# Splitting hid once and using more seven-product pairs in an encoder block's channel mixer

## The chip, the cores and the metric

The kernel runs on one core of one Trainium2 chip. The time is the device time of one execution in microseconds (us); several executions are taken and the median is given. A core has TensorE (PE, matrix products; PEld is its weight load), VectorE (DVE), ScalarE (ACT), GpSimd (POOL), a sequencer that here issues almost all DMAs (SP), and 16 DMA engines. Engines work side by side, each through its own instructions in a fixed order, and wait for each other by semaphores. Operands lie in SBUF, 128 partitions wide; PE writes to PSUM, whose banks hold 512 float32 columns.

## The reference

One layer of an encoder on 256 positions of width 2048, all float32. The two parts that the change touches most are the channel mixer and the norm behind it:

```
hn = rmsnorm(h, ffn_norm_pre)
up = hn @ w_ffn_up                        # 2048 -> 2 x 5632
gate, val = split(up)
gate = dwconv_centred(gate, 3 taps, bias) # along positions
ff = (gelu(gate) * val) @ w_ffn_down      # 5632 -> 2048
h = h + rmsnorm(ff, ffn_norm_post)        # rmsnorm: y * rsqrt(mean(y*y) + EPS) * g
```

Ahead of it stand a combined input projection, a bidirectional state-space mixer beside a pooling mixer, and an output projection (w_out), with norms around them. Behind it stands a gate: `h + rmsnorm(sigmoid(rmsnorm(h) @ w_gate) * (p @ w_ple))`.

## The kernel before

**Products in three parts.** To keep float32 accuracy at the speed of a reduced format, each operand is split into a high part (a rounding copy on ACT, `split`, line 149) and a low part (the rest, a subtraction on DVE, line 150). A product is then high x high + high x low + low x high: three matmuls. Weights come from HBM by DMA in pieces of 1 MB into one of three `raw` buffers of 2048 columns, are split 1024 columns at a time into one of five `whi` and five `wlo` buffers, and used once.

**Stages.** In order: dtu, xbc and z (the input projection, with the state-space and pooling work put between its matmuls), wo (the output projection), ple (the small projection of p; its first half here), up, down (called dn), ple's second half, and gt (the gate).

**up.** `feature_pairs` makes 256 of the 5632 gate or value features for all 256 positions. Per k (128 of the 2048 input rows) and per 128 features there is one matmul of 512 columns (the high weight against both parts of the input) and one of 256 (the low weight against the high part). `total` adds the two halves of each bank. A slab is 512 gate and 512 value features; there are 11. After a slab's gate features come `conv` (three taps: one ACT and two DVE instructions for each 128 features), gelu on ACT, and a multiplication by the row scale `rfb` on POOL (line 781), because the pre-norm's row scale is applied behind the projection. The products gate x value go to six pages `hid` in float32.

**down.** `sublayer` runs two halves of 1024 output columns. `token_major` walks through 22 pairs of row blocks (2 x 128 rows of w_down). An ordinary pair has 24 matmuls of 512 columns. For the pairs named in `fast` it calls `seven_products`: a 2 x 2 block product with seven block products in place of eight (21 matmuls), for which DVE makes sums and differences of the weight blocks, and `hid_sums` those of hid. hid is split again in each half, pair by pair (`get_hid`, lines 797 and 798); the sums of four pairs are kept from the first half to the second, the others are made anew. The four accumulators of the ordinary products are in `acc`, those of the shared block products in `alt`; `combine` adds them after the last seven-product pair. At the end of a half, ACT squares each accumulator (for the norm) and DVE multiplies it by the gain; after both halves POOL makes the row scale, DVE adds to the residual `h` (line 740), and PE turns the result for the gate's products (`panel_part`).

**What sets the order.** The program names engines and data; a planner puts the instructions of every engine, and SP's DMAs, into one fixed order by its own estimate of times, with program order as the priority, and hands out buffers as they come free. So the split of a later weight piece can stand ahead of or behind the work of a handover. `load` puts a DMA behind the last weight load, unless it is called with `ahead`.

**Room.** 13 pages of 2048 columns, 3 buffers `mid` of 1024, 6 PSUM banks handed out singly (`main`) and 2 more (`misc`).

## Time and profile before

| what | value |
|---|---|
| median of 3 runs | 1144.95 us (1144.41 to 1144.95) |
| profiled execution's span | 1144.3 us |
| mean granted TensorE clock | 0.994 of full speed |
| busy: PE, PEld, DVE, ACT, POOL | 1127.1, 970.4, 818.4, 614.2, 79.3 us |
| DMA moved | 219.04 MB, mean 191 GB/s |

| stretch, us from the span's start | stage |
|---|---|
| 0 to 53 | dtu |
| 53 to 150 | xbc |
| 150 to 206 | z |
| 206 to 296 | wo |
| 296 to 330 | ple's first half, handover to up |
| 330 to 798.6 | up |
| 798.6 to 1031.5 | down |
| 1031.5 to 1052 | handover to the gate |
| 1052 to 1144.3 | gate and output |

The profile shows one execution. A group's row gives the number of instructions, their busy time and the mean of one in ns, then the time that the engine was idle just before them and what ended it. A row of the timeline gives start and duration. Ends of matmuls are modelled, so a matmul's duration in a row is longer than the pace at which they follow each other; pace is read from starts. A table by stretches gives the busy time of each engine in each, the granted clock, the DMA engines' share and their rate.

### The profile page before, as it was taken

Reading aid. Unit: us, or ns where it says so; the run is one execution under the profiler, and the core shown is the slowest. Engines: PE = TensorE matmul, PEld = TensorE weight load, DVE = VectorE, ACT = ScalarE, POOL = GpSimd, SP = SyncE. Lnnn points to the kernel's source line nnn. Section 1 sums busy time; section 2 is a strip of 40 time slices with the busy share of each in tenths; the row PEclk is TensorE's granted clock in tenths of the full one; section 3 lists DMA queues with packets and bytes.
Section 4 is the critical chain, followed back from the end, with each engine's and each line's share of the span. In section 5 each row is a group of like instructions: output and inputs, shape, how many; then the busy total and the mean of one; then the engine's idle time right before and its main releaser. Section 6 shows DMA issues by size and latency. Waiting matters only on the chain.

```text
span 1144.3 us, 15384 instructions
## 1 busy us (share of the span) xinstructions
PE 1127.1 (98%) x6049; PEld 970.4 (85%) x6049; DVE 818.4 (72%) x1067; ACT 614.2 (54%) x837; POOL 79.3 (7%) x91
## 2 busy tenths in 40 slices
PE   9999999999999999999999999999999999999996
PEld 9998888888888888888888888888888888887885
DVE  6659985754876666665766756668888888898573
ACT  6746543553674554554544545545655655667462
POOL 0201105200110000000000000000000000002001
PEclk9999999999999999999999999999999999999998
DMA  9942366556456555555555555556556746654752
GB/s 357 374 149 74 100 245 221 171 170 198 148 185 214 190 185 184 184 187 194 193 190 193 184 184 184 184 195 220 170 188 220 221 147 221 209 195 147 226 179 74
DMA packets 129592, 219.04 MB, mean 191 GB/s; under 512 B 3696, under 2 KB 96752, under 8 KB 128624
## 3 DMA queue, kind: packets, MB, share of 16 engines
q1 hardware_dynamic: 129232, 217.70, 57.2%
q8 instruction: 47, 0.77, 0.3%
q10 hardware_dynamic: 288, 0.36, 0.1%
q14 instruction: 25, 0.20, 0.0%
HBM read 215.95 MB, written 2.10 MB: 191 GB/s over the span
## 4 chain that ended last, share of the span: by engine, by line
PE 95%; DVE 2%; ACT 1%; POOL 1%; issue 1%; DMA 0%; POOLq 0%; DVEq 0%; ACTq 0%
PE va L86 21%; PE ga L86 21%; PE dna L86 17%; PE woa L86 8%; PE gt L86 7%; PE xbc L86 5%; PE dtu L86 4%; PE z L86 4%; PE dns L86 3%; PE pw L86 1%; PE ple L86 1%; PE yd L86 0%; DVE h L740 0%; PE seg L86 0%; DMA dtur<-w_in 0%
## 5 line engine op out<-in xcount | busy, mean ns | idle before, releaser
L86 PE MATMUL ga<-wox,ug_0h 128*128 128x512 f32 x352 | 125.5, 395 | 0.0
L86 PE MATMUL ga<-wox,ug_1h 128*128 128x512 f32 x352 | 125.1, 394 | 0.0
L86 PE MATMUL va<-wox,uv_0h 128*128 128x512 f32 x352 | 124.8, 393 | 0.0
L86 PE MATMUL va<-wox,uv_1h 128*128 128x512 f32 x352 | 124.8, 393 | 0.0
L86 PE MATMUL ga<-wox,ug_0l 128*128 128x256 f32 x352 | 99.1, 282 | 0.0
L86 PE MATMUL ga<-wox,ug_1l 128*128 128x256 f32 x352 | 99.1, 282 | 0.0
L86 PE MATMUL va<-wox,uv_0l 128*128 128x256 f32 x352 | 99.1, 281 | 0.0
L86 PE MATMUL va<-wox,uv_1l 128*128 128x256 f32 x352 | 99.1, 281 | 0.0
L86 PEld LDWEIGHTS va<-wox,uv_0h 128*128 128x128 f32 x352 | 66.1, 188 | 15.0
L86 PEld LDWEIGHTS va<-wox,uv_1h 128*128 128x128 f32 x352 | 66.1, 188 | 15.0
L86 PEld LDWEIGHTS ga<-wox,ug_1h 128*128 128x128 f32 x352 | 66.1, 188 | 14.9
L86 PEld LDWEIGHTS ga<-wox,ug_0h 128*128 128x128 f32 x352 | 66.1, 188 | 14.8
L86 PE MATMUL dna<-dn_0h,hs 128*128 128x512 f32 x248 | 75.8, 393 | 0.0
L86 PE MATMUL dna<-dn_1h,hs 128*128 128x512 f32 x248 | 75.6, 393 | 0.0
L86 PEld LDWEIGHTS ga<-wox,ug_0l 128*128 128x128 f32 x352 | 66.2, 188 | 0.1
L86 PEld LDWEIGHTS ga<-wox,ug_1l 128*128 128x128 f32 x352 | 66.2, 188 | 0.0
L86 PEld LDWEIGHTS va<-wox,uv_0l 128*128 128x128 f32 x352 | 66.2, 188 | 0.0
L86 PEld LDWEIGHTS va<-wox,uv_1l 128*128 128x128 f32 x352 | 66.2, 188 | 0.0
L781 POOL TENSOR_TENSOR fc<-fc,rfb 128x1024 f32<-128x1024 f32 x11 | 26.5, 2408 | 440.1 <-ACT fc L780 440.1
L86 PEld LDWEIGHTS dna<-dn_1h,hs 128*128 128x128 f32 x248 | 46.5, 188 | 10.8
L86 PEld LDWEIGHTS dna<-dn_0h,hs 128*128 128x128 f32 x248 | 46.5, 188 | 10.7
L86 PE MATMUL dna<-dn_0l,hs 128*128 128x512 f32 x124 | 40.2, 393 | 0.0
(1078 smaller groups left out, 2824.0 us busy)
## 6 DMA issues: line engine op xcount, KB each, us to landing
dn0r<-w_ffn_down SPq DMA_DIRECT2D x22, 1024.0 KB, 5.5
dn1r<-w_ffn_down SPq DMA_DIRECT2D x22, 1024.0 KB, 5.5
zr<-w_in SPq DMA_DIRECT2D x8, 1024.0 KB, 5.1
wo0r<-w_out SPq DMA_DIRECT2D x8, 1024.0 KB, 5.4
wo1r<-w_out SPq DMA_DIRECT2D x8, 1024.0 KB, 5.4
gt0r<-w_ple_gate SPq DMA_DIRECT2D x8, 1024.0 KB, 5.6
gt1r<-w_ple_gate SPq DMA_DIRECT2D x8, 1024.0 KB, 5.5
dtur<-w_in SPq DMA_DIRECT2D x14, 528.0 KB, 8.9
```

The source lines that it names most:

```text
L86: nc.tensor.matmul(o, lhsT, rhs, start=start, stop=stop, skip_group_check=True)
L781: nc.gpsimd.tensor_tensor(cv.rearrange("p (f t) -> p f t", f=4), cv.rearrange("p (f t) -> p f t", f=4), rfb.unsqueeze(1).to_broadcast([P, ...
```

## The change

- **hid.** gate x value goes to a `mid` buffer and is split once, in up, into a high and a low part: five pairs of pages and a smaller pair. `get_hid` is gone. For the pairs that down treats with seven products, DVE makes the sums of hid's blocks in up, too; they are stored to HBM, and each half of down loads and splits them.
- **Pairs.** Every second pair up to the twentieth is a seven-product pair, ten in each half, 20 in all; before it was six and seven. The block sums are taken in another form, into `mid` buffers and not in place.
- **Norm.** The values are no longer multiplied by `rfb`. The row scale of the pre-norm cancels in the norm behind down, except in its EPS, which becomes EPS times the pre-norm's mean square (`fmean`, passed as `base`).
- **Splits.** `whi` and `wlo` are three buffers of 2112 columns, and a 2048-column piece is split in one instruction on each engine; the first piece of a `token_major` stage and of up in steps of 512, 512 and 1024; `feature_major` in two steps as before.
- **Taps.** up's convolution makes its three products on ACT, 12 instructions a slab, and DVE adds them with two instructions of 1024 columns.
- **PSUM.** `main` buffers are pairs of banks, three of them; up's `total` works on 512 columns at once.
- **Room.** 14 pages, 5 `mid` buffers; gains are loaded into pages; h and one half of the gated projection's input are stored to HBM at up's start and loaded again, h at the thirteenth pair of down's second half and the other after down; the scratch space for DMA descriptors is smaller.

```
-            tc.tile_pool(name="pmain", bufs=6, space=bass.MemoryType.PSUM) as pm, \
+            tc.tile_pool(name="dram", bufs=1, space=bass.MemoryType.DRAM) as dp, \
+            tc.tile_pool(name="pmain", bufs=3, space=bass.MemoryType.PSUM) as pm, \
...
-            return gp.tile([P, 2048], dtype, tag="pg", bufs=13, name=name)
+            return gp.tile([P, 2048], dtype, tag="pg", bufs=14, name=name)
...
-            return gp.tile([P, 1024], dtype, tag="mid", bufs=3, name=name)
+            return gp.tile([P, 1024], dtype, tag="mid", bufs=5, name=name)
...
         def main(name):
-            return [pm.tile([P, 512], F32, tag="main", name=f"{name}_{i}") for i in range(2)]
+            t = pm.tile([P, 1024], F32, tag="main", name=name)
+            return [t[:, :512], t[:, 512:]]
...
-        def split(name, src, nel, cuts=()):
+        def parts(name):
             if name in spare:
-                hi, lo = spare.pop(name)
-            else:
-                hi = wp.tile([P, 1056], F32R, tag="whi", bufs=5, name=f"{name}h")
-                lo = wp.tile([P, 1056], F32R, tag="wlo", bufs=5, name=f"{name}l")
-            for c0, c1 in zip((0, *cuts), (*cuts, nel)):
+                return spare.pop(name)
+            return [wp.tile([P, 2112], F32R, tag=tag, bufs=3, name=f"{name}{tag}") for tag in ("whi", "wlo")]
+
+        def split(dst, src, c0, *cuts):
+            hi, lo = dst
+            for c1 in cuts:
                 s = slice(c0, c1)
                 last["act"] = ins(nc.scalar.copy(hi[:, s], src[:, s]))
                 last["dve"] = ins(nc.vector.tensor_sub(lo[:, s], src[:, s], hi[:, s].bitcast(F32)))
+                c0 = c1
...
         def seven_products(name, r, a_, acc, alt, start, stop):
             v = r.rearrange("p (b c) -> p b c", b=4)
-            b11 = split(f"{name}a", r[:, :512], 512)
-            b2 = split(f"{name}b", r[:, 1024:], 1024)
-            nc.vector.tensor_sub(v[:, 0:2], v[:, 1::2], v[:, 0:2])
-            nc.vector.tensor_sub(v[:, 3], v[:, 3], v[:, 0])
-            nc.vector.tensor_sub(v[:, 2], v[:, 2], v[:, 3])
-            t13 = split(f"{name}c", r[:, :1024], 1024)
-            t42 = split(f"{name}d", r[:, 1024:], 1024)
+            f, g = mid(f"{name}f"), mid(f"{name}g")
+            nc.vector.tensor_sub(f.rearrange("p (b c) -> p b c", b=2), v[:, 1:3],
+                                 v[:, 0].unsqueeze(1).to_broadcast([P, 2, 512]))
+            nc.vector.tensor_add(g[:, :512], v[:, 2], f[:, :512])
+            nc.vector.tensor_sub(g[:, 512:], v[:, 3], g[:, :512])
+            b = split(parts(f"{name}b"), r, 512, 2048)
+            t = parts(f"{name}t")
+            for x, c in ((f, slice(0, 1024)), (g, slice(1024, 2048))):
+                split([y[:, c] for y in t], x, 0, 1024)
...
-                for j in range(2):
-                    group.append((k0 + j, *split(f"{name}{k0}_{j}", r[:, j * 1024:(j + 1) * 1024], 1024)))
+                wh, wl = split(parts(f"{name}{k0}"), r, 0, *((512, 1024, 2048) if u == 0 else (2048,)))
+                group.extend((k0 + j, wh[:, j * 1024:(j + 1) * 1024], wl[:, j * 1024:(j + 1) * 1024]) for j in range(2))
...
         def total(o, acc):
-            for f in range(2):
-                nc.scalar.copy(o[:, f * L:(f + 1) * L], acc[f][:, L:])
-                nc.vector.tensor_add(o[:, f * L:(f + 1) * L], o[:, f * L:(f + 1) * L], acc[f][:, :L])
+            v, w = o.rearrange("p (f t) -> p f t", f=2), acc.rearrange("p (f q t) -> p q f t", f=2, q=2)
+            nc.scalar.copy(v, w[:, 1])
+            nc.vector.tensor_add(v, v, w[:, 0])
...
+        def taps(name, x, wcol, bcol):
+            o, t0, t2 = (mid(f"{name}{i}") for i in range(3))
+            for f in range(4):
+                c = slice(f * L, (f + 1) * L)
+                nc.scalar.activation(t0[:, c], x[:, c], AF.Copy, scale=vec(wcol + f))
+                nc.scalar.activation(t2[:, c], x[:, c], AF.Copy, scale=vec(wcol + 2 * NF + f))
+                nc.scalar.activation(o[:, c], x[:, c], AF.Identity, bias=vec(bcol + f), scale=vec(wcol + NF + f))
+            o4, a4, b4 = (z.rearrange("p (f t) -> p f t", f=4) for z in (o, t0, t2))
+            nc.vector.tensor_add(o4[:, :, 1:], o4[:, :, 1:], a4[:, :, :L - 1])
+            nc.vector.tensor_add(o4[:, :, :L - 1], o4[:, :, :L - 1], b4[:, :, 1:])
+            return o
...
         def gload(name, src):
-            g = cp.tile([P, D], F32, tag="gain", name=name)
+            g = page(name)
             load(g, src.partition_broadcast(P))
...
-            r = [rms(f"{name}{t}", sq[t], 1.0 / D) for t in range(2)]
+            r = [rms(f"{name}{t}", sq[t], 1.0 / D, 1, base[t]) for t in range(2)]
...
+        fmean = [cp.tile([P, 1], F32, name=f"fmean{t}") for t in range(2)]
+        for t in range(2):
+            nc.gpsimd.tensor_scalar(fmean[t], means["rf", t], EPS, None, op0=ALU.mult)
...
+        def put_away():
+            for n, t in (("h0", h[0]), ("h1", h[1]), ("pl0", pl[0])):
+                nc.sync.dma_start(away[n], t)
...
+        seven = [u for u in range(NF // 2) if u % 2 == 1 and u < 21]
+        sums = {u: dp.tile([P, 512], F32, name=f"sums{u}") for u in seven}
...
+        def block_sums(u, x):
+            s = mid(f"hs{u}")
+            a11, a21, a12, a22 = (x[:, i * P:(i + 1) * P] for i in range(4))
+            s1, s2, s3, s4 = (s[:, i * P:(i + 1) * P] for i in range(4))
+            nc.vector.tensor_add(s1, a21, a22)
+            nc.vector.tensor_sub(s3, a11, a21)
+            nc.vector.tensor_sub(s2, s1, a11)
+            nc.vector.tensor_sub(s4, a12, s2)
+            stores.append(lambda: nc.sync.dma_start(sums[u], s[:, :512]))
...
-            cv = conv(f"fc{s}", sc, 3, V_FCW + 4 * s, NF, V_FCB + 4 * s)
+            cv = taps(f"fc{s}", sc, V_FCW + 4 * s, V_FCB + 4 * s)
             nc.scalar.activation(cv, cv, AF.Gelu_apprx_tanh)
-            nc.gpsimd.tensor_tensor(cv.rearrange("p (f t) -> p f t", f=4), cv.rearrange("p (f t) -> p f t", f=4),
-                                    rfb.unsqueeze(1).to_broadcast([P, 4, L]), op=ALU.mult)
...
+                if 2 * s + i in seven:
+                    block_sums(2 * s + i, hd)
+            for c0, c1 in ((0, 512), (512, 1024)) if s == DFF // 512 - 1 else ((0, 1024),):
+                split((hh, hl), hv, c0, c1)
...
         def hid_sums(k):
+            s, o = mid(f"sums{k}"), mid(f"hs{k}", F32R)
+            load(s[:, :512], sums[k // 2], True)
+            split((o[:, 512:], o), s, 0, 512)
...
-                      fast=((2, 5, 8, 11, 14, 17), (2, 5, 8, 11, 14, 17, 19)), sums=hid_sums)
+                      fast=(seven, seven), sums=hid_sums, base=fmean,
+                      hooks={12: lambda: hb.extend(bring_back(f"h{t}") for t in range(2))})
+        h = hb
+        pl = [bring_back("pl0")]
```

More of the change, by code (lines that the diff above doesn't have):

```diff
@@ L317, in rms @@
             nc.gpsimd.tensor_tensor(r, m, mhalf[:, :n], op=ALU.pow)
+            last["mean"] = m
             return r
@@ L341, in row_rstd @@
                 r.append(rms(f"{name}{t}", [q], 1.0 / D))
+                means[name, t] = last["mean"]
             return r
@@ L413, in build @@
                 with tc.issue_after(front[0]), tc.issue_after(front[1]):
-                    wh, wl = split(f"dtu{k}", r[j][:, :1056], 1056, ((352, 704), (704,))[k] if k < 2 else ())
+                    if j == 0:
+                        both = parts(f"dtu{k}")
+                    wh, wl = split([x[:, j * 1056:] for x in both], r[j], 0,
+                                   *(((352, 704), (704,))[k] if k < 2 else ()), 1056)
                 if k == 8:
@@ L884, in build @@
                 for i in (8, 6):
-                    sh, sl = page(f"gth{i}", F32R), page(f"gtl{i}", F32R)
-                    for j in range(2):
-                        spare[f"gt1{NK - i}_{j}"] = (sh[:, j * 1024:(j + 1) * 1024], sl[:, j * 1024:(j + 1) * 1024])
+                    spare[f"gt1{NK - i}"] = page(f"gth{i}", F32R), page(f"gtl{i}", F32R)
             token_major(f"gt{half}", w_gate, half * 1024, list(range(NK)), hp, acc, 1 + 3 * half)
```

145 lines of the change are left out of this document (67 added, 78 removed).

## The prediction

> **What bounds the kernel now.** Read first the page's busy shares and its chain.
>
> ```profile
> span 1144.3 us, 15384 instructions
> PE 1127.1 (98%) x6049; PEld 970.4 (85%) x6049; DVE 818.4 (72%) x1067; ACT 614.2 (54%) x837; POOL 79.3 (7%) x91
> ...
> PE va L86 21%; PE ga L86 21%; PE dna L86 17%; PE woa L86 8%; PE gt L86 7%; PE xbc L86 5%; PE dtu L86 4%; PE z L86 4%; PE dns L86 3%; PE pw L86 1%; PE ple L86 1%; PE yd L86 0%; DVE h L740 0%; PE seg L86 0%; DMA dtur<-w_in 0%
> ```
>
> TensorE (PE) is busy 98% of the span, and the chain of what ended last runs almost wholly through its matmuls. Work on another engine can only matter where PE waits for it. So read next the table by stretches: up (330 to 798.6 us), the two halves of down, and four microseconds of the handover from down to the gate.
>
> ```profile
> core 0: us, PE busy (x) PEld busy (x) DVE busy (x) ACT busy (x) POOL busy (x), PEclk, DMA share, GB/s
> 330.00:798.60 468.60, 468.60 (x2687) 411.33 (x2686) 315.55 (x401) 235.76 (x313) 26.49 (x11) 1.00 0.58 191
> 798.60:916.40 117.80, 117.80 (x511) 95.72 (x511) 102.89 (x128) 69.53 (x90) 0.91 (x2) 1.00 0.61 197
> 916.40:1031.50 115.10, 115.10 (x500) 93.50 (x499) 99.87 (x114) 68.50 (x86) 0.14 (x1) 1.00 0.59 192
> 1045.00:1049.00 4.00, 4.00 (x15) 3.43 (x16) 2.92 (x6) 1.61 (x4) 0.00 (x0) 0.57 0.69 213
> ```
>
> In up PE is never without work, while VectorE (DVE) works 315.55 of 468.60 us and ScalarE (ACT) 235.76: a third and half of them are free. In down DVE is at 87% (102.89 of 117.80), the highest of any engine beside PE. Third, whom PE waited for:
>
> ```profile
> PE gt L86 <- DVE gt_1l L150: 2.3, 1, 2.3
> PE xbc L86 <- DVE xb_0l L150: 2.0, 1, 2.0
> ```
>
> These are the two longest waits. Behind the first one the granted clock of the row 1045 to 1049 is 0.57, so the wait of 2.3 us costs (1 - 0.57) x 4.0 = 1.7 us more, 4.0 together.
>
> **The change, part by part.**
>
> *Pairs.* The chain in order of time shows down's opening: two ordinary pairs of row blocks, then one seven-product pair.
>
> ```profile
> 798.58 11.11 PE dna L86 x48
> 809.68 0.69 PE dns L86 x3
> ...
> 814.53 1.62 PE dna L86 x7
> ```
>
> Forty-eight matmuls take 11.11 us, 5.55 us for a pair of 24. The seven-product pair is 21 matmuls, from 809.68 to 814.53, 4.85 us. One more such pair saves 0.70 us of PE. The old lists hold 6 and 7 pairs, the new one 10 for each half: 7 more, 7 x 0.70 = 4.9 us, all on the path, since PE has no idle time in either half. Term: -4.9 us. Nothing else in the change removes a matmul.
>
> *Does DVE keep up in down?* Its instructions overlap at their ends, so I take start to start.
>
> ```profile
> 1008.32 1.23 DVE L150 TENSOR_TENSOR dn_0l<-dn1r,dn_0h 128x1024 fp32r<-128x1024 f32 x1 [1.55 <-ACT dn_0h L149]
> 1009.46 1.22 DVE L150 TENSOR_TENSOR dn_1l<-dn1r,dn_1h 128x1024 fp32r<-128x1024 f32 x1
> 1010.60 0.68 DVE L798 TENSOR_TENSOR hs<-hid,hs 128x512 fp32r<-128x512 f32 x1
> 1011.20 0.69 DVE L150 TENSOR_TENSOR dn138al<-dn1r,dn138ah 128x512 fp32r<-128x512 f32 x1
> ```
>
> So 1024 columns cost 1.14 us and 512 cost 0.60. No 2048-column instruction is in the trace; it lies between 1.14 + 1.08 (the added 1024 columns at the slope of these two rows) = 2.22 and twice 1.14 = 2.28, and I take 2.22; 1536 columns are 1.68 likewise. An ordinary pair was 2 x 1.14 for weights and 0.60 for hid, 2.88; it becomes 2.22. A seven-product pair was 0.60 + 1.14 (first parts) + 1.14 + 0.60 + 0.60 (differences) + 2 x 1.14 = 6.36, and 0.60 for hid, and 0.60 plus four small sums where these were not kept. It becomes 1.14 + 2 x 0.60 + 1.68 + 2 x 1.14 + 0.60 (split of the loaded sums) = 6.90. A half is then 10 x 6.90 + 12 x 2.22 + 12 x 0.60 (combine and the four drains) = 102.8 us against PE's 10 x 4.85 + 12 x 5.55 = 115.1, 89%. That is the present share, spread more evenly, since pairs of the two kinds now alternate. I take no new wait. Without that cover each uncovered microsecond would be one of the span.
>
> *What goes to up.* It loses the multiplication on POOL and six of eight narrow DVE instructions per slab; it gains eight ACT instructions, two DVE adds, a split and one set of block sums.
>
> ```profile
> L781 POOL TENSOR_TENSOR fc<-fc,rfb 128x1024 f32<-128x1024 f32 x11 | 26.5, 2408 | 440.1 <-ACT fc L780 440.1
> ...
> L369 ACT ACTIVATE fc<-gr,vt 128x256 f32<-128x256 f32 x44 | 24.0, 592 | 0.0
> L375 DVE SCALAR_TENSOR_TENSOR fc<-gr,vt,fc 128x255 f32<-128x255 f32 x88 | 36.6, 478 | 0.0
> L798 DVE TENSOR_TENSOR hs<-hid,hs 128x512 fp32r<-128x512 f32 x44 | 30.1, 685 | 0.1
> L826 DVE TENSOR_TENSOR hd<-hid x9: 281/284/291, 768.4 to 916.4; 128x128 f32<-128x128 f32 x9
> ```
>
> DVE per slab: 8 x 0.478 = 3.8 goes; 2 x 1.14 + 1.14 + 4 x 0.28 = 4.5 comes, 11 x 0.7 = 8 us on 315.55 of 468.60. ACT: 88 x 0.592 = 52 us for the taps and 11 x 1.05 for splits (the first row of the next fence), together 64 on 235.76; 300 of 468.60 stays covered. Twelve taps and the gelu hold ACT for 8.2 us in one burst, from some 2 us after a slab's last gate matmul. PE takes 32 matmuls a chunk, 468.60 / 2687 x 32 = 5.6 us, so the next weight buffer comes free 3.6 us into the burst and its split starts 4.6 us late; with its own 4.2 us (next part) it ends 8.8 us after its buffer came free, and PE wants it after two more chunks, 11.2. Cost 0, gain 0: POOL waited 440 us for this work and nobody waited for POOL.
>
> *Weights 2048 at a time.* ACT repeats 1024 columns every 0.95 us:
>
> ```profile
> 1020.51 1.04 ACT L149 CAST dn_0h<-dn1r 128x1024 fp32r<-128x1024 f32 x1
> 1021.46 1.04 ACT L149 CAST dn_1h<-dn1r 128x1024 fp32r<-128x1024 f32 x1
> ```
>
> A chunk goes through ACT in about 2.0 and DVE in 2.22, and its first low half is there only after 4.2 us instead of 1.05 + 1.14 = 2.2. In the steady state prefetch covers this. At a handover, where small urgent instructions stand beside a split, one of them can wait up to 2.22 - 1.14 = 1.1 us more. From wo to up I put 0.3 for that, 0.2 for the combines, which now both stand just ahead of a half's end. Term: +0.5, ends 0 and +2.2.
>
> *From down to the gate.* The wait of 2.3 us has these rows:
>
> ```profile
> 1033.03 1.05 ACT L149 CAST gt_1h<-gt0r 128x1024 fp32r<-128x1024 f32 x1
> ...
> 1043.67 1.22 DVE L150 TENSOR_TENSOR gt_1l<-gt0r,gt_1h 128x1024 fp32r<-128x1024 f32 x1
> ```
>
> The high half was done at 1034.1, but DVE took the low half up only at 1043.67, behind the residual and the panel, because its buffer came free only with the end of down. With three whole buffers the gate's first chunk gets the one of the next to last pair, 5.55 us earlier, and DVE has lost two hid splits there. Ends: the wait stays and another 2.22 split comes ahead of it, +2.2; wait and slow clock both go, -4.0. Neither end has a row of the new order, so I take the middle of 0 and -4.0: -2.0. This row also weighs a rule. The Trainium skill, "TensorE: Matmul & The Clock Gate", Part 1, says that the clock halves after at least one idle window of about 3.4 us. The trace differs: a wait of 2.3 us had 0.57 behind it. By the rule the term would be at most -2.3, with the row it is -4.0.
>
> *Transfers.* Storing and loading h, one half of the gated projection and the sums adds 3 + 3 + 10 x 0.25 + 20 x 0.25 = 13.5 MB to 219.
>
> ```profile
> DMA packets 129592, 219.04 MB, mean 191 GB/s; under 512 B 3696, under 2 KB 96752, under 8 KB 128624
> ...
> dn0r<-w_ffn_down SPq DMA_DIRECT2D x22, 1024.0 KB, 5.5
> gffn<-ffn_norm_post SPq DMA_DIRECT2D x1, 1024.0 KB, 7.8
> ```
>
> ```profile
> 290.82 7.97 SPq L118 DMA_DIRECT2D ug01r<-w_ffn_up  x2
> 310.36 0.37 SPq L118 DMA_DIRECT2D uv00r<-w_ffn_up  x1
> 507.72 5.96 SPq L118 DMA_DIRECT2D ug50r<-w_ffn_up  x2
> ```
>
> ```profile
> 305.71 0.74 DVE L740 SCALAR_TENSOR_TENSOR h<-wom,wo1r,h 128x512 f32<-128x512 f32 x1
> 519.34 1.05 ACT L149 CAST ug_0h<-ug50r 128x1024 fp32r<-128x1024 f32 x1
> 846.82 0.62 ACT L149 CAST dn022ah<-dn0r 128x512 fp32r<-128x512 f32 x1 [0.19 <-DMA dn0r<-w_ffn_down]
> ```
>
> Between 299 and 310 SP issues nothing, and h is final at 306.5: there the stores go out. In up a load issued at 507.72 and landing 5.5 us later is used at 519.34, 6.1 us to spare; a store of sums waits on SP for DVE, ahead of the loads behind it, a few microseconds. In down loads are used as they land (0.19 us waited), but PE did not wait. A seven-product pair's raw buffer now comes free after its first differences and not after the last split. The gain vector's load needs a page that comes free with up's last matmul; if it stood on SP ahead of all of down's loads, PE would wait 5.5 + 1.05 + 0.6 = 7.2 us; loads already in the three raw buffers cover 16. Cost 0, ends 0 and +7.
>
> **Sum.** -4.9 - 2.0 + 0.5 = -6.4. The profiled execution has 1144.3, the median of the runs is 1144.95, 0.6 us around the span; 1144.95 - 6.4 = 1138.5.
>
> **Rivals.** *DVE's order in down (slower).* An ordinary pair's low half is wanted 4.85 + 4 x 0.23 = 5.8 us after its buffer came free. ACT 2.0 + DVE 2.22 fits, also behind the next pair's differences (1.14 + 1.20 + 2.22 = 4.6). Behind its 1536-column split as well it is 6.2, 0.5 us late; 20 times that is 10 us: 1144.95 - 4.9 + 10 = 1150. From 0.25 us a pair (4.9 / 20) the gain is gone. DVE's 87% and the load without slack speak for it; that PE never waited in down under 9 us bursts speaks against it. *A new handover wait (no difference).* One more wait of 2.2 us with its slow clock takes 3.9 back: 1143.9. The two present ones show the price; that most handovers run without speaks against it. *SP blocked at down's start:* 1144.95 - 4.9 + 7 = 1147. *Work moved, nothing saved:* if PE's pairs were not the bound, 1145; the stretch rows exclude most of it.
>
> **How the numbers follow.** My forecast, from 1144.95 - 4.9 - 4.0 = 1136.0 to 1144.95 - 4.9 + 0.5 + 2.2 = 1142.7 by the ends of the gate's term, 0.60; better still, the 2.0 us wait at xbc gone too (1134.0), 0.06; no difference 0.13; slower, DVE's order 0.16 and SP 0.05. About 0.2%, 2.3 us, is what can be told from no change: 1142.7 and 1147.2. Faster 0.66, same 0.13, slower 0.21. The range 1134 to 1148 leaves out most of the 0.16 for DVE's order.
>
> **What would show it.** Right: down's two halves take 115 us each, PE full, DVE near 89%; up stays at 468.6 with POOL empty; no PE wait on gt_1l and the clock at 1.00 there. Wrong: PE waits in down on the low half of ordinary pairs, a gap at up's end with SP waiting for a page, or new waits on 2048-column splits at the handovers.

## The result and the profile after

The changed kernel takes 1157.53 us (median of four runs, 1153.33 to 1160.88) against 1144.95: the ratio is 1.011, with an interval of 1.008 to 1.014. It is 12.6 us slower where 6.4 us of gain were forecast, and it lies outside the range of 1134 to 1148.

The page of the changed kernel, its first lines:

```profile
span 1153.0 us, 14754 instructions
...
PE 1124.5 (98%) x6028; PEld 966.2 (84%) x6028; DVE 797.6 (69%) x821; ACT 620.8 (54%) x720; POOL 59.8 (5%) x82
```

PE did 21 matmuls fewer, DVE is less busy than before, and the profiled execution (1154.79 us, span 1153.0) is 8.7 us longer than that of before (span 1144.3). (A run's time is some 1.8 us above its span, so the execution profiled before took some 1146.1 us, a little above its median.) The page alone would not tell why. The stages do; each time is from the first matmul of a stage to that of the next, worked out from the traces. The last column is the first experiment, told below.

| stage, us | before | after | difference | 1024-column splits |
|---|---|---|---|---|
| up to xbc | 52.8 | 53.8 | +1.1 | 53.8 |
| xbc and z | 153.2 | 149.4 | -3.8 | 149.8 |
| wo | 90.6 | 89.0 | -1.6 | 89.0 |
| ple, handover to up | 32.8 | 41.9 | +9.2 | 35.5 |
| up | 469.1 | 465.9 | -3.1 | 465.9 |
| down | 235.1 | 242.8 | +7.7 | 229.3 |
| handover, gate, output | 110.8 | 110.2 | -0.6 | 107.8 |

So there are two losses, at the handover to up and in down, and small gains in stages that the change was not expected to touch. The gain in xbc and z is in the main a wait that is gone: before, PE waited 2.0 us for `xb_0l`, and 3.41 us at half clock behind that cost 1.7 more; in the changed kernel no wait in xbc is above 0.2 us, and the clock there is full. The gains in wo and up have another source, told below. The table by stretches of the changed kernel shows where PE stood (first the part of the handover that waits, then up, down's first half, and the second half in three pieces):

```profile
core 0: us, PE busy (x) PEld busy (x) DVE busy (x) ACT busy (x) POOL busy (x), PEclk, DMA share, GB/s
...
300.00:334.12 34.12, 28.67 (x158) 25.05 (x157) 20.79 (x30) 21.03 (x34) 2.02 (x6) 0.90 0.57 203
334.12:800.04 465.92, 465.92 (x2691) 410.82 (x2690) 297.99 (x247) 257.26 (x278) 0.00 (x0) 1.00 0.61 198
800.04:915.29 115.25, 110.19 (x476) 88.28 (x475) 96.39 (x85) 62.72 (x55) 0.00 (x0) 1.00 0.64 207
...
926.00:940.00 14.00, 11.81 (x37) 8.54 (x36) 10.85 (x12) 6.21 (x6) 0.00 (x0) 0.76 0.62 217
940.00:1042.84 102.84, 102.34 (x441) 81.95 (x440) 89.18 (x83) 58.49 (x55) 0.50 (x1) 1.00 0.71 224
```

Up is full, as before. At the handover PE is idle for 34.12 - 28.67 = 5.5 us and the clock falls to 0.90 of full in the mean. In down's first half PE is idle for 5.1 us of 115.25. In 926 to 940 it is idle for 2.2 us, and the clock stands at 0.76; so the loss there comes in two parts, as at the gate before. The view of whom PE waited for, in the changed kernel (us in total, times, longest):

```profile
PE woxt L335 <- DVE wox L194: 4.6, 2, 4.0
PE dna L91 <- ACT hs L156: 1.4, 1, 1.4
PE dna L91 <- DVE dn016wlo L157: 1.4, 1, 1.4
...
PE gt L91 <- DVE gt02wlo L157: 1.1, 1, 1.1
...
PE dna L91 <- DVE dn020wlo L157: 0.6, 1, 0.6
```

The longest wait is one on the panel of the handover (`wox`), then one on the split block sums (`hs`), and a family of waits on low halves of ordinary pairs, one at each second pair. Each is read from its rows.

**The handover.** The timeline of the changed kernel, DVE first, then ACT, then PE (start, duration, instruction, in brackets the idle time ahead of it and what ended it):

```profile
306.14 2.28 DVE L157 TENSOR_TENSOR ug010wlo<-ug01r,ug010whi 128x2048 fp32r<-128x2048 f32 x1
308.34 0.87 DVE L194 SCALAR_TENSOR_TENSOR wox<-woxt,vt,wox 128x256 fp32r<-128x256 f32 x2
311.16 2.29 DVE L157 TENSOR_TENSOR ug011wlo<-ug01r,ug011whi 128x2048 fp32r<-128x2048 f32 x1 [1.95 <-ACT ug011whi L156]
313.37 0.87 DVE L194 SCALAR_TENSOR_TENSOR wox<-woxt,vt,wox 128x256 fp32r<-128x256 f32 x2
...
309.23 1.90 ACT L156 CAST ug011whi<-ug01r 128x2048 fp32r<-128x2048 f32 x1 [1.57 <-PE ga L91]
...
313.99 1.94 PE L335 MATMUL woxt<-ident,h 128*128 128x128 f32 x8 [4.03 <-DVE wox L194]
```

DVE's order has a split of 2048 columns ahead of the panel's small instruction. That split waits for ACT's copy, which waits until PE frees a weight buffer. So the panel stands 1.95 us behind a DVE that does nothing and then 2.29 us behind the split, although its own 0.87 us of work was needed first. PE waits 4.03 us.

**Down's first half.** The chain of what ended last in the changed kernel, two rounds of it (one round is an ordinary pair and a seven-product pair):

```profile
819.35 2.30 DVE dn08wlo L157
...
821.67 5.97 DMA dn0r<-w_ffn_down
...
827.73 1.24 DVE dn014f L215
...
828.99 0.70 DVE dn014g L217
...
830.32 2.29 DVE dn012wlo L157
...
832.63 6.90 DMA dn0r<-w_ffn_down
```

PE isn't in it: the chain is a loop of DVE and loads. The low half of an ordinary pair (830.32) ends the use of a `raw` buffer; only then does the next load go out; that load brings the seven-product pair whose first difference (`f`, then `g` twice) DVE takes up; and behind these in DVE's order stands the low half of the ordinary pair that PE already waits for. One round is 830.32 to 842.22 here, 10.97 the round before; 24 + 21 matmuls at 0.227 us are 10.2.

**The half change.** SP's DMAs in the changed kernel, then ACT's and PE's first use of what they bring:

```profile
919.14 0.37 SPq L123 DMA_DIRECT2D dn1r<-w_ffn_down  x1
919.60 0.42 SPq L123 DMA_DIRECT2D h_back<-h_away  x1
920.07 4.42 SPq L123 DMA_DIRECT2D sums<-sums  x2
...
928.44 0.62 ACT L156 CAST hs<-sums 128x512 fp32r<-128x512 f32 x1 [4.29 <-DMA sums<-sums]
...
929.11 0.50 PE L91 MATMUL dna<-dn12bwhi,hs 128*128 128x512 f32 x1 [1.42 <-ACT hs L156]
```

The sums, 0.25 MB, are issued behind 2 MB of weights and h, and are used 8.4 us after their issue. PE waits 1.42 us. What follows that wait, and the one at the handover, is a slow clock (the table by stretches, granted clock in the third column from the right):

```profile
313.00:320.00 7.00, 6.01 (x22) 5.41 (x23) 3.08 (x7) 4.88 (x9) 0.00 (x0) 0.51 0.66 223
930.80:937.70 6.90, 6.13 (x15) 4.80 (x15) 6.90 (x7) 3.85 (x4) 0.00 (x0) 0.51 0.62 192
```

Two stretches of 7 us at half speed. Each costs some 3.4 us, on top of the waits ahead of it (4.0 us, and 1.4 and 0.8 us).

One thing is needed to read the times below: executions of the changed kernel and its relatives fall into two groups some 6 to 9 us apart, most clearly where that is said; where it can be seen, it is up that differs.

### The profile page after: what moved, and what is told of

Its sections match the earlier page's. It is cut to its first block, busy times and chain, and to the rows that moved or that the text cites. A ratio compares the mean times of both kernels' runs of the same rounds, so it can differ in the third digit from the quotient of the medians.

```text
span 1153.0 us, 14754 instructions
## 1 busy us (share of the span) xinstructions
PE 1124.5 (98%) x6028; PEld 966.2 (84%) x6028; DVE 797.6 (69%) x821; ACT 620.8 (54%) x720; POOL 59.8 (5%) x82
## 4 chain that ended last, share of the span: by engine, by line
PE 77%; DVE 11%; DMA 6%; ACT 3%; issue 2%; POOL 1%; DVEq 0%; SPq 0%; POOLq 0%; ACTq 0%
PE ga L91 21%; PE va L91 21%; PE woa L91 8%; PE dna L91 7%; PE gt L91 7%; DMA dn0r<-w_ffn_down 4%; PE z L91 4%; PE dtu L91 3%; PE xbc L91 2%; PE dns L91 2%; DMA sums<-sums 1%; DVE cv L399 1%; DVE w L627 1%; PE yd L91 1%; DVE h_back L768 0%
## 5 line engine op out<-in xcount | busy, mean ns | idle before, releaser
L373 ACT ACTIVATE fc<-gr,vt 128x256 f32<-128x256 f32 x44 | 25.9, 589 | 0.0
L371 ACT ACTIVATE fc<-gr,vt 128x256 f32<-128x256 f32 x44 | 22.0, 499 | 0.0
L372 ACT ACTIVATE fc<-gr,vt 128x256 f32<-128x256 f32 x44 | 21.8, 497 | 0.0
L399 DVE SCALAR_TENSOR_TENSOR cv<-xr,vt,cv 128x254 f32<-128x254 f32 (+1 forms) x48 | 19.7, 474 | 0.0
L157 DVE TENSOR_TENSOR hs<-sums,hs 128x512 fp32r<-128x512 f32 x20 | 13.7, 686 | 3.7 <-ACT hs L156 3.7
L841 DVE TENSOR_TENSOR gr<-gr,rfb 128x512 f32<-128x512 f32 x22 | 15.2, 692 | 0.8
L375 DVE TENSOR_TENSOR fc<-fc,fc 128x1020 f32<-128x1020 f32 x11 | 13.4, 1221 | 3.3 <-ACT fc L373 3.3
L856 DVE TENSOR_TENSOR hv<-hv,fc 128x512 f32<-128x512 f32 x22 | 15.2, 692 | 0.7
L315 DVE TENSOR_TENSOR hv<-hv,va 128x512 f32<-128x512 f32 x22 | 15.0, 681 | 0.6 <-ACT hv L314 0.6
L315 DVE TENSOR_TENSOR gr<-gr,ga 128x512 f32<-128x512 f32 x22 | 15.0, 680 | 0.0
L376 DVE TENSOR_TENSOR fc<-fc,fc 128x1020 f32<-128x1020 f32 x11 | 13.4, 1221 | 0.4
L314 ACT COPY gr<-ga 128x512 f32<-128x512 f32 x22 | 12.7, 577 | 0.0
L314 ACT COPY hv<-va 128x512 f32<-128x512 f32 x22 | 12.6, 571 | 0.0
L848 ACT ACTIVATE fc<-fc 128x1024 f32<-128x1024 f32 x11 | 11.6, 1056 | 0.0
```

Source lines behind the costliest of these rows:

```text
L157: last["dve"] = ins(nc.vector.tensor_sub(lo[:, s], src[:, s], hi[:, s].bitcast(F32)))
L314: nc.scalar.copy(v, w[:, 1])
L315: nc.vector.tensor_add(v, v, w[:, 0])
L371: nc.scalar.activation(t0[:, c], x[:, c], AF.Copy, scale=vec(wcol + f))
L372: nc.scalar.activation(t2[:, c], x[:, c], AF.Copy, scale=vec(wcol + 2 * NF + f))
L373: nc.scalar.activation(o[:, c], x[:, c], AF.Identity, bias=vec(bcol + f), scale=vec(wcol + NF + f))
```

## The experiments

Three theories stood at the start. A: single instructions of 2048 columns hold up DVE's and ACT's fixed orders. B: the order of the pairs, twenty of them evenly spaced, is too much for DVE. C: the added DMAs (h ahead of the sums) cost the time. The stages with unexpected gains were open. (The recorded expectations give their theories letters of their own, run by run.)

**All splits at 1024 columns again** (`e1`; the rest of the change stays):

```
-  split(parts(f"{name}{k0}"), r, 0, *((512, 1024, 2048) if u == 0 else (2048,)))        # token_major
+  split(parts(f"{name}{k0}"), r, 0, *((512, 1024, 2048) if u == 0 else (1024, 2048)))
-  ... (512, 1024, 2048) if name == "ug00" and u == 0 else (2048,)                        # feature_pairs
+  ... (512, 1024, 2048) if name == "ug00" and u == 0 else (1024, 2048)
```

> Edit: every weight chunk of up, down, wo, ple and gate is split in two pieces of 1024 columns again; buffers, pairs and all else as changed. Theory A (single 2048-column instructions stand in front of the small urgent ones at the handover from wo to up, and VectorE's order holds the low half back in down): the handover, from the first ple matmul to the first value matmul, falls from 41.9 us to 33 to 35; the waits of 0.5 to 0.8 us on an ordinary pair's low half in down's first half shrink, since the first half chunk is there 1.1 us earlier, but the time of that half falls by no more than 3 us; up goes from 22.19 us per 128 matmuls back to 22.33, +3 us. Total 1143 to 1149. Theory B (the handover is long because banks are handed out in pairs or because of the stores to HBM): it stays at 40 to 42 and the total at 1153 to 1161. Theory C (down is short of VectorE time): down gets longer still, by 10 x 0.06 us and more.

Measured: 1133.29 us (1132.94 to 1134.05), ratio to before 0.990 [0.989, 0.992]. It is 24 us faster than the changed kernel and 11.7 faster than the kernel before, and below all that was expected (1143 to 1149 by the theory that came nearest). Its waits and its halves of down:

```profile
PE woxt L335 <- DVE wox L194: 1.2, 1, 1.2
...
PE dna L91 <- ACT hs L156: 0.9, 1, 0.9
```

```profile
793.94:904.12 110.18, 110.18 (x488) 91.25 (x487) 99.42 (x101) 64.81 (x67) 0.00 (x0) 1.00 0.69 223
904.12:1023.24 119.12, 117.52 (x512) 95.40 (x511) 107.13 (x112) 68.44 (x80) 2.25 (x4) 1.00 0.73 235
```

The waits on low halves in the first half are gone, the clock stays at 1.00, and DVE does no less work (206.55 us in the whole of down, against 205.46). The halves can't be compared by their times alone: their border is the first matmul with a weight of the second half, and here 486 matmuls stand ahead of it, in the changed kernel 474. Up keeps its new length, though its splits are as before: its gain has another source.

**Where the long splits cost** (`e5`: 1024 columns in up's first slab alone; `e6`: in down's ordinary pairs alone).

```
+  ... else (1024, 2048) if name in ("ug00", "ug01") else (2048,)         # e5, feature_pairs
+  ... else (1024, 2048) if name[:2] == "dn" else (2048,)                 # e6, token_major
```

> Edit: of the changed kernel, only the weight chunks of up's first gate features (four of them) are split 1024 columns at a time; all others stay at 2048. Theory A (the handover is long because of these few instructions alone): from the first ple matmul to the first value matmul 35 to 36 us against 41.9, the half clock there gone, down as in the changed kernel (242 to 247); total 6 to 8 us below the changed kernel, 1145 to 1153. Theory B (a later queue or the stores to HBM make it long): 40 to 42 and 1153 to 1161.

> Edit: of the changed kernel, only down's ordinary pairs are split 1024 columns at a time; up, wo, ple and gate stay at 2048. Theory A (down's waits come from the single 2048-column low half behind the next pair's differences, and the late sums between the halves follow from that lateness): down 229 to 232 us against 242.8, the handover stays at 41 to 42; total 1138 to 1146. If the lateness between the halves has its cause in the load of h alone, 5 us stay there: down 235 to 237, total 1143 to 1151. This run and the one with the first slab alone should add up to what all chunks at 1024 gave (20 to 24 us below the changed kernel).

Measured: `e5` 1146.03 us (1144.86 to 1148.05), `e6` 1144.24 (1142.75 to 1154.94), each as fast as the kernel before within 0.35%. By stages `e5` takes 35.5 us at the handover in place of 41.9, and nothing in down; `e6` takes 232.8 us in down in place of 242.8, and nothing at the handover. So both places are A's, 6.4 and 10 us of span, 16.5 of the 21.9 by which `e1`'s span is shorter. `e1` has 3.5 us less in down than `e6`, where short waits on low halves remain, and 0.8 less from down's end to the last matmul; two things that I did not take apart further.

**The pairs and the order** (`e2`: the old lists of seven-product pairs; `e3`: the first difference of a pair is put behind the low half of the ordinary pair ahead of it, the 2048-column splits stay).

```
-  seven = [u for u in range(NF // 2) if u % 2 == 1 and u < 21]           # e2
+  seven = [2, 5, 8, 11, 14, 17, 19]      # and fast=(seven[:6], seven)
+  with tc.issue_after(last["plain"]):                                    # e3, around the difference f
```

> Edit: the lists of seven-product pairs are the old ones (six and seven), with their block sums made in up; all else as changed. Theory A (a loop of load, differences and low half on VectorE's fixed order costs 11.1 us for each two alternating pairs, where TensorE needs 10.4): with two ordinary pairs between, the loop has 5.5 us more and the waits of down's first half go; down's two halves take 118 and 117 us plus the wait of about 5.6 us between them, 240 to 241 against 242.8. Total 1151 to 1158. Theory C (too much VectorE work in down in sum): the same picture, but VectorE's busy share in down falls from about 85% to below 80%. Theory D (the extra transfers slow every load): the loads still take 6.1 us and waits stay, down 247 and more.

> Edit: one ordering edge: the first difference of a seven-product pair comes behind the low half of the ordinary pair before it on VectorE; not one instruction more or less. Theory A (VectorE stands waiting for the next pair's load with the low half, which TensorE needs, queued behind it): down's first half falls from 115.3 us with 6.5 us of waits to 109 to 110, the second half's 1.4 us of small waits go; down in all 235 to 237 against 242.8; total 1147 to 1154, and the spread between runs shrinks. Theory C (VectorE is short of time) and theory D (loads too slow): no change, since work and transfers are the same; down 241 to 244.

Measured: `e2` 1151.26 us, ratio 1.006 [1.005, 1.008]; `e3` 1151.55 (1151.29 to 1161.61), ratio 1.008 [1.005, 1.011]. With the old lists there are still waits, now on the low halves behind the fewer pairs:

```profile
PE dna L91 <- DVE dna L237: 1.6, 1, 1.6
PE dna L91 <- DVE dn012wlo L157: 1.6, 1, 1.6
PE dna L91 <- DVE dn018wlo L157: 1.2, 1, 1.2
```

B falls for the first half: fewer pairs and a less busy DVE do not remove the waits. That half takes 122.7 us for 510 matmuls, some 7 us above 0.227 us for each, as in the changed kernel (115.25 for 474). My expectation that they would go was wrong. What does shrink is the loss in the second half, from some 9 to some 3 us: there the first seven-product pair comes a pair later, and PE no longer waits for `hs`. `e3` shows that the waits come from the order:

```profile
849.17 2.29 DVE L157 TENSOR_TENSOR dn016wlo<-dn0r,dn016whi 128x2048 fp32r<-128x2048 f32 x1 [1.34 <-ACT dn016whi L156]
...
853.12 1.22 DVE L216 TENSOR_TENSOR dn018f<-dn0r 128x1024 f32<-128x1024 f32 x1
```

The low half (`dn016wlo`) now stands ahead of `f`. The chain of what ended last runs almost wholly through PE's matmuls in that half and no longer through loads; PE is idle there for 0.5 us and not 5.1, and the half takes 110.94 us in place of 115.25 for the same 474 matmuls. The handover stays as it was. The half change is no better: PE waits 3.4 us for `hs`, and 6.83 us at half clock follow.

**h behind the weights** (`e4`: h is loaded again behind the last weight load; `e14`: the same in `e1`).

```
-  load(t, away[n], True)
+  load(t, away[n], ahead)                 # ahead=False for h
```

> Edit: the two loads that bring h back stand behind the weight load of the thirteenth pair of down's second half on the DMA queue; nothing else. Theory A (the first load of sums of the second half is issued behind a 1 MB load of h, takes 8.3 us, ScalarE waits 4.3 us for it in its fixed order, TensorE waits and its clock halves for 6.8 us): the 5.6 us lost between 926 and 940 us fall to 0 to 2; total 3 to 5 us below the changed kernel, 1149 to 1156. Theory E (that load of sums is late anyway, since it stands behind a weight load that waits for its buffer): 4 us or more stay lost there.

> The version with 1024-column splits (1133.29) with h loaded again behind the last weight load and not ahead of the sums. Theory (the load of h ahead of the sums costs only where the loop of raw buffers is late, as with 2048-column splits): no stall at the half change is left to save, 1132 to 1133.5. Rival (the place in the queue costs in itself): down's second half shorter by 4 or more, 1128 to 1129.

Measured: `e4` 1145.82 us (1144.26 to 1148.32), ratio to before 1.001 [1.000, 1.002]; down's second half takes 120.73 us and not 127.55, so C is right in that place, and by more than I expected. SP's rows of `e4`, and the first use:

```profile
916.72 0.37 SPq L123 DMA_DIRECT2D dn1r<-w_ffn_down  x1
917.18 4.91 SPq L123 DMA_DIRECT2D sums<-sums  x2
...
923.31 0.62 ACT L156 CAST hs<-sums 128x512 fp32r<-128x512 f32 x1 [1.58 <-DMA sums<-sums]
```

The sums are used 6.1 us after their issue, not 8.4. But `e14` is at 1132.76 (1132.47 to 1133.14), half a microsecond below `e1`: with 1024-column splits h's place costs next to nothing. `e6`, too, has h ahead of the sums, and its second half takes 118.0 us (510 matmuls, 12 fewer than in `e4`). So the loss at the half change needs both, the 2048-column splits in down and h in the queue; taking either away saves it. I had put the first of the two down to the late loop of the first half. `e3` speaks against that: its first half is not late, and its half change loses as much. The losses are not independent, and the savings of single experiments do not add up.

**The price of the pairs** (`e1` with the old lists, so that nothing else waits).

> The version with 1024-column splits (1133.29) with the old lists of seven-product pairs (six and seven, 13 in all, not 20). It prices the prediction's first term where nothing waits. By that term: 7 x 0.70 = 4.9 us slower, 1138.2, all of it in down. Rival (the seven more pairs bring less, because their sums and loads cost elsewhere): 1133 to 1136.

Measured: 1137.71 us (1136.54 to 1139.1) against 1133.29: 4.4 us for seven pairs. In down it is 233.38 against 229.30, 4.1 us.

**The unexpected gain.** In wo the same products are made from the same data, and in up almost the same ones, and yet they take less time. In equal stretches of up (300 us) and wo (50 us) the changed kernel fits more matmuls. First before, then after:

```profile
400.00:700.00 300.00, 300.00 (x1722) 263.32 (x1720) 197.18 (x243) 148.57 (x197) 16.87 (x7) 1.00 0.57 187
230.00:280.00 50.00, 50.00 (x219) 40.61 (x218) 26.22 (x26) 22.37 (x30) 0.48 (x2) 1.00 0.60 189
```

```profile
400.00:700.00 300.00, 300.00 (x1733) 264.54 (x1732) 188.78 (x156) 164.77 (x178) 0.00 (x0) 1.00 0.60 196
230.00:280.00 50.00, 50.00 (x222) 41.40 (x222) 25.17 (x20) 20.69 (x21) 1.11 (x2) 1.00 0.60 190
```

PE is busy throughout and the granted clock is 1.00 in all four, so neither waits nor the clock explain it. Two parts of the change could be tried alone in the kernel before: PSUM buffers in pairs of banks (`f1`), and the smaller descriptor space (`f2`).

```
-  tc.tile_pool(name="pmain", bufs=6, ...)      # f1; main() then hands out halves of a [P, 1024] tile
+  tc.tile_pool(name="pmain", bufs=3, ...)
+  dynamic_dma_scratch_size=1024                # f2
```

> Edit: the kernel before, with its six single PSUM banks handed out as three pairs of banks, as in the changed kernel; nothing else. In the changed kernel 512-column matmuls follow each other every 227 ns in wo and down, in the kernel before every 231, whatever the splits. Theory P (the pair of banks makes that pace): 227 ns here too, about 10 to 12 us less over wo, up, down and gate, total 1133 to 1136. Theory Q (it is another part: the place of the operands in SBUF, the buffers' width, the smaller scratch space): 231 ns and 1144 to 1147.

> Edit: the kernel before, with the smaller scratch space for DMA descriptors, which moves where everything lies in SBUF; nothing else. Theory Q1 (the operands' place makes the matmuls' pace): 227 ns between 512-column matmuls and 1133 to 1136. Otherwise 231 ns and 1144 to 1147.

Measured: `f1` 1147.73 us, ratio 1.003 [1.002, 1.004]; `f2` 1145.19, ratio 1.0005 [0.9996, 1.0015]; in both, 128 matmuls of up take 22.33 us, as before (after: 22.19). Neither is the source. (`f1` shortens what follows down by 2.4 us, where PE waits 0.4 us on `gt_1l` and not 2.3, and lengthens the handover to up by 3.5.)

Single matmuls tell more. In the gate's last stretch before there is almost no DMA and little other work, and still some matmuls are longer than others, always the same ones (start, duration):

```profile
1126.92 0.39 PE L86 MATMUL gt<-gt_0h,dnxh 128*128 128x512 f32 x1
1127.14 0.40 PE L86 MATMUL gt<-gt_0l,dnxh 128*128 128x512 f32 x1
1127.38 0.39 PE L86 MATMUL gt<-gt_0h,dnxl 128*128 128x512 f32 x1
1127.60 0.40 PE L86 MATMUL gt<-gt_1h,dnxh 128*128 128x512 f32 x1
1127.84 0.39 PE L86 MATMUL gt<-gt_1l,dnxh 128*128 128x512 f32 x1
```

From start to start: 0.22, 0.24, 0.22, 0.24. What tells these matmuls apart is the place in SBUF of the operand that streams through PE, here the split weights. (The places are those that the program gives out; the trace has no addresses.) The ten `whi` and `wlo` buffers of the kernel before are 1056 columns wide, 4224 bytes, which is 33 x 128: every second buffer lies 128 bytes off the others' 256-byte step. In the gate's last 22 us:

| streamed operand, address modulo 256 | matmuls | ns to the next |
|---|---|---|
| 96 (as the pages), after another with 96 | 33 | 226 or 227 |
| 96, after one with 224 | 17 | 226 |
| 224, after one with 96 | 17 | 234 |

That is a hint and not the rule. In wo and down of the kernel before, where much else runs, the matmuls follow every 229 to 233 ns in the mean wherever the operands lie, and every 231 from one at 96 to the next at 96. And in up the streamed operand is always at 96; there it is the loaded weights that lie on and off the step, and up is slower, too. The changed kernel's buffers are 2112 columns, 8448 bytes, 33 x 256: all lie on one step. So I widened the buffers of the kernel before (`f3`), and set those of `e1` off the step (`g1`):

```
-  hi = wp.tile([P, 1056], F32R, tag="whi", bufs=5, ...)          # f3 (lo the same), on f2
+  hi = wp.tile([P, 1088], F32R, tag="whi", bufs=5, ...)
-  wp.tile([P, 2112], F32R, tag=tag, bufs=3, ...)                 # g1, on e1
+  wp.tile([P, 2144], F32R, tag=tag, bufs=3, ...)
```

> The kernel before with one size changed: the ten buffers of split weights are 1088 columns wide and not 1056 (4352 bytes, a multiple of 256, in place of 4224, which is 33 x 128), and the small descriptor space, which alone made no difference (1145.19), to make room. Theory L (the place of the split weights in SBUF sets the matmuls' pace): in the gate's tail before, each matmul that reads a buffer 128 bytes off the others was followed after 234 ns, all others after 226 or 227; with all buffers on one 256-byte step the 512-column matmuls follow every 226.7 ns in z, wo, down and gate, up takes 22.19 us per 128 matmuls and not 22.33 (21 x 0.15 = -3.1 us), xbc and z -3.8, wo -1.6, down some 1000 x 4.5 ns = -4.5: 1131 to 1133. Rival (the pace comes from something else in the change, or of the execution): 1145, pace 231.

> The version with 1024-column splits (1133.29) with one size changed: the six buffers of split weights are 2144 columns wide and not 2112 (8576 bytes, 67 x 128, so that every second buffer lies 128 bytes off the 256-byte step, as in the kernel before). Theory L: the pace of before comes back, 231 ns between 512-column matmuls and 22.3 us per 128 in up: 1133.3 + 13 = 1146, no other stage change. Rival: 1133, pace 227.

Measured: `g1` 1142.33 us (1141.09 to 1144.3), 9.0 slower than `e1`. `f3` falls into two groups, 1134.0 to 1137.3 (five of twelve runs) and 1143.0 to 1145.0 (seven), with a median of 1143.05 and a ratio of 0.996 [0.994, 0.998]; its profiled execution is one of the first group, 1134.36 with a span of 1132.6, 11.7 us under that of before. (Of these, 1.7 us are not the pace: the wait at xbc is there, without a slow clock behind it.) I had expected 1131 to 1133 for all runs. The same two stretches, `f3` first, then `g1`:

```profile
400.00:700.00 300.00, 300.00 (x1733) 262.36 (x1732) 199.07 (x246) 149.72 (x197) 16.88 (x7) 1.00 0.58 190
230.00:280.00 50.00, 50.00 (x222) 41.42 (x221) 25.61 (x25) 22.56 (x29) 0.50 (x2) 1.00 0.60 191
```

```profile
400.00:700.00 300.00, 300.00 (x1725) 263.73 (x1724) 189.99 (x211) 169.17 (x233) 0.00 (x0) 1.00 0.59 192
230.00:280.00 50.00, 50.00 (x218) 40.62 (x217) 24.96 (x28) 21.54 (x30) 0.46 (x2) 1.00 0.59 186
```

One width, changed in either direction, moves the pace with it: 1733 and 222 with the buffers on one step, 1725 and 218 off it. That the width of these buffers, and with it their place, sets the pace is shown. That the 256-byte step is what counts fits the two widths on it and the two off it; no width off by another amount was tried. I expected 13 us from `g1` and got 9.

The second group is in part explained by `e3`, whose profiled execution was its longest, 1161.61 against 1151.3 to 1153.9 for the others:

```profile
400.00:700.00 300.00, 300.00 (x1700) 260.07 (x1699) 184.86 (x153) 160.23 (x171) 0.00 (x0) 1.00 0.59 193
```

With all buffers on one step, up's alternating matmuls of 512 and 256 columns settle at its start into one of two patterns, 346.7 or 353.4 ns for the two together (22.19 or 22.61 us per 128), and stay there: of the ten profiles with all buffers on one step, nine hold 22.19 and that of `e3` 22.61. Up's 2816 matmuls make that 9 us, the distance of `f3`'s groups. For `f3` this is an inference, since its slow group has no profile. What decides between the patterns is open, and so is the spread of the changed kernel itself (two runs near 1154, two near 1160.5), which is smaller.

## Why the prediction was wrong

**Pairs, -4.9: right.** 4.4 us where nothing else waits (`g2` against `e1`). With matmuls at 0.227 us the same working gives 4.8.

**2048-column splits, +0.5, ends 0 and +2.2: this is the step that failed.** The measured price is the difference of `e1` and the changed kernel, 21.9 us of span: 6.4 at the handover to up (41.9 - 35.5), 13.5 in down (242.8 - 229.3), 2.3 from down's end to the last matmul, and 0.3 the other way elsewhere. The working counted how much longer one instruction is than another, 1.1 us for a single delay. Three things were not in it. A long instruction in a fixed order also waits for its own input, and with it all behind it (1.95 us idle plus 2.29 at the handover). With three whole buffers in place of five halves that input comes later, since PE must be done with 2048 columns before ACT may write. `e1` keeps the three buffers and waits only 1.2 us there, so they alone are not the loss. And behind the wait of 4.0 us the clock stood at half for 6.83 us (for 3.41 in `e2` and `e4`, behind the same wait), which the prediction had priced for the gate, but not for new waits.

**DVE keeps up in down, cost 0: wrong, and the rival had the place.** It said that an ordinary pair's low half stands behind the next pair's differences. It does. But the rival made its price from a fixed lateness (0.5 us a pair, 10 us, 1150) and dismissed the case without the 1536-column split as fitting, 4.6 of 5.8 us. The chain shows why it doesn't fit: the differences wait for a load that goes out only when the low half ahead has freed its `raw` buffer, so 2.29 + 6.0 + 1.24 + 1.4 us close to a loop of 11 to 12 us against 10.2 of matmuls. DVE's work was forecast well, 205.46 us in down against 2 x 102.8. Its share (84% in the first half; I had 89%) says nothing of the loop: DVE is idle in it while the load flies. The waits on the low halves of ordinary pairs, and new ones at a handover, are two of the signs of being wrong that the prediction named. That loads were used as they landed was quoted in the prediction, as a point for the rival; it was the sign to follow further, by asking what had let each load go out.

**Transfers, cost 0, ends 0 and +7: the upper end came.** Putting h behind the weights shortens down's second half by 6.8 us. I looked for the danger at down's start, in the gain vector's load; it was at the half change, where h goes out ahead of the sums. That 6.8 comes so near to 7 is chance: the 7 was a price for another wait.

**The gate, -2.0: right in size where the splits are short, by a way that is not shown.** The wait on the first low half was 2.3 us with a slow clock behind it; after, it is 1.1 on `gt02wlo` and 0.9 on ACT, at full clock. From down's end to the last matmul `g1`, which has 1024-column splits and the old pace, takes 99.5 us against 101.7, a gain of 2.2. Two runs say that this need not be the three whole buffers, to which the prediction gave it. `f1`, which has the banks in pairs and the old buffers, takes 99.3. And `f2`, with the old wait of 2.2 us but the clock at full behind it, takes 100.3: some 1.5 us of the gain are a slow clock that does not follow this wait each time. In the changed kernel it is 100.9, of which the new pace accounts for 0.8 (`f3` has 100.9, too): the longer splits took the gain back. On the rule weighed there: the Trainium skill, "TensorE: Matmul & The Clock Gate", Part 1, has the clock judged in free-running windows of about 3.4 us. The slow stretches in the clock's record are 3.41 us long in the kernel before and 6.83, twice that, in the changed one, behind waits of 4.0 and of 1.4 and 0.8 us. That the lengths are whole windows agrees; that so short a wait is enough does not fit a window without any work. Nor does the length of a wait alone decide here: 2.2 us left the clock at full in `f2`, 2.3 did not in the kernel before.

**Up stays, cost 0 for what moves there: right in its place, for wrong numbers.** PE is full in up and POOL has 0.00, but DVE went down, from 315.55 to 297.99 us, where I had 8 us more, and ACT is at 257 and not 300. Up itself is shorter by 3.1 us, from the pace.

**Left out: the pace.** It is worth 9.0 us (`g1` against `e1`). Without it the changed kernel would have been slower still. The prediction has no term for the buffers' new width.

**The wait at xbc: the rival with 0.06 came about.** It is gone in the changed kernel, and `g1`, at the old pace, takes 2.8 us less for xbc and z than the kernel before. Which part of the change took it away is not shown.

So 1133.3, the time of `e1`, is 1144.95 - 4.4 for the pairs - 9.0 for the pace, plus 1.8 for what remains. That is a remainder and not a sum: the handover to up is 2.7 us longer than before (`f1`, with the banks in pairs alone, has 3.5, which points at them), the waits at xbc and at the gate are shorter, and the profile of before is of an execution above the median (the prediction set its span, 1144.3, beside the median, 1144.95, without the 1.8 us between a span and its time). The long splits bring it to 1157.5.

## What to carry to other kernels

Fewer and longer instructions on an engine that is not the bound were no saving here: in a fixed order each was a block that small urgent work stood behind, together with that block's own wait for input. Before such a merge, follow the chain of one round in the stage (buffer freed, load out, load landed, first use, next buffer freed) and compare its length with the bound engine's time for that round; the busy share does not show it. And when stages that compute the same get faster or slower, look at where operands lie: a buffer width that keeps all of them on one 256-byte step was worth more here (9.0 us) than the seven more pairs (4.4).

## What was not expected of the hardware

- Matmuls of 512 columns in wo follow each other every 226.7 ns when all split buffers lie on one 256-byte step (`f3`, `e1`, `after`), and every 230.9 to 231.1 ns in the mean when they alternate by 128 bytes (`before`, `g1`), with the same granted clock of 1.00. Why the place has this effect is not shown.
- Up's alternating matmuls hold one of two patterns for the whole stage, 22.19 us per 128 in nine profiles and 22.61 in one, when the buffers lie on one step; with buffers off the step they take 22.3 in each of the four profiles (`before`, `f1`, `f2`, `g1`). That the pattern is chosen anew in each execution is an inference from the spread of the times.
- The same wait does not cost the same each time. Behind 2.0 us at xbc the clock stood at half for 3.41 us in `before` and `f2`, and at full in `f1` and `f3`; behind 2.2 to 2.3 us at the gate at half in `before` and `f3`, and at full in `f2`; behind 4.0 us at the handover at half for 6.83 us in `after` and 3.41 in `e2` and `e4`. Waits of 1.4 and 0.8 us within five microseconds brought the clock to half for 6.83 us; in `e1` a single wait of 1.2 us left it at full.
